# Turning the keys' lower parts of both attention maps together, and moving the scale and parts of w_o's last block

## The chip, the cores and the metric

The kernel runs on one core of one Trainium2 chip. The metric is the device time of one execution in microseconds (us), as the median of several runs.

## The reference

One step of a hybrid encoder layer: 1024 new frames of a prompt and 32 frames of a running stream (with 512 cached keys and values) go through differential attention and retention, are merged and multiplied with w_o, and pass a gated feed-forward and a gated per-layer embedding. D_MODEL is 1024, there are 8 heads of each kind. Each attention head has two maps of width 64. What matters here:

```python
def mix_inputs(x, w_in, g_norm, g_qn, g_kn, pos):
    h = rmsnorm(x, g_norm)
    z = h @ w_in
    qa, ka, va, qr, kr, vr, g_ret, gate_a, gate_r = jnp.split(z, splits, axis=-1)
    qa = rmsnorm(qa.reshape(B, T, A_HEADS, 2, A_DIM), g_qn)
    ka = rmsnorm(ka.reshape(B, T, A_HEADS, 2, A_DIM), g_kn)
    ...

def diff_attn_prompt(qa, ka, va, lam):
        s = jnp.einsum('bqhcd,bkhcd->bhcqk', q_blk, ka).astype(jnp.float32) * scale
        p = jax.nn.softmax(jnp.where(mask, s, -jnp.inf), axis=-1)
        a = p[:, :, 0] - lam * p[:, :, 1]
        return jnp.einsum('bhqk,bkhe->bqhe', a.astype(va.dtype), va)

def merge_and_tail(x, o_a, o_r, gate_a, gate_r, p, w_o, g_ffn, w_ff_gate, w_ff_up,
                   w_ff_down, g_ple, w_ple, w_ple_gate):
    mix = jax.nn.sigmoid(gate_a) * o_a + jax.nn.sigmoid(gate_r) * o_r
    x = x + mix @ w_o
    h = rmsnorm(x, g_ffn)
    x = x + (jax.nn.silu(h @ w_ff_gate) * (h @ w_ff_up)) @ w_ff_down
    gate = jax.nn.sigmoid(rmsnorm(x, g_ple) @ w_ple_gate)
    return x + gate * (p @ w_ple)
```

## The kernel before

All large products are made of fp16 pairs: a matrix is scaled and split into a high part and a lower part (value minus high part), and a product is high x high, high x low and low x high, added up in PSUM (`mm3`, L473). The tokens are 1056 columns, in 9 tiles (8 of 128 and one of 32).

**Stage A** runs over 8 heads x 9 tiles. For each unit it projects the tile (L734 to L736, 24 products of 512 columns for each of two weight pairs), and `unit_a` (L1011) takes queries and keys of both maps. It normalises them, casts the high parts to fp16 (L1060, L1061), subtracts for the lower parts (L1063, L1064), turns six 128x128 groups on PE into one PSUM bank (L1072) and copies them out: four groups with the keys to `kT` (L1077) and two with the queries to `q4` (L1081; both in the helper at L388). Group 0 and 1 hold a map's high and lower query parts side by side, so one product over 128 rows multiplies both with the keys' high part, which stands twice in the rows (64 rows each); a second product with the keys' lower part (L878) completes the scores. For this the kernel keeps `kT[:, 0:2]` (high parts of the two maps, doubled) and `kT[:, 2:4]` (lower parts, doubled), and so for the 512 cached keys in `kcs` (L846 to L854). `attend` (L864) makes scores, softmax and the product with the values; `unit_b` (L1182) makes retention and the merged rows.

**The seam.** In the last head, `load_ple`, `load_wo_0` and `load_wo_1` load the per-layer embedding's and w_o's weights: w_o in four blocks of 256 columns (0 and 1 in one weight tile, 2 and 3 in another). `load_block_steps` (L392) loads a block to one of two staging tiles, takes four reductions for the largest value (L426), multiplies by the rows' scale and reduces again (L429, L435), lets PE turn the column of maxima and spread it (L275, L286 in `spread_max`), and derives the scale. `split_block` (L449) then makes the parts, eight pairs of one ACT and one DVE instruction (L459, L461). For block 3 the kernel stops after the scale (`hold`), and the split is done in the next stage. Beside this run the products of the per-layer embedding (PLE, L474 to L476 into `pj`, copied out at L1354 and stored at L1360 and L1362).

**Stage BC** (`stream_bc`, L1796) first makes the products with w_o: four chunks of tokens (352, 352, 176, 176 columns) x 8 column blocks m of 128, each 8 x 3 products. `residual` (L1540) loads `xf` by DMA (L1546), adds each product to it (L1553), stores it, sums squares (L1561, L1564), and makes the norm (PE at L1572 and L1587, then L1591) and the operands of the feed-forward (L1501, L1507, and the sums for a product scheme of 7 in place of 8). `load_gu` (L1613) prepares the feed-forward's weights. Then come gate and up, the down product, and at last the embedding's gate.

**What sets the order.** PE, DVE, ACT and POOL execute in the order in which the program issues, and that order is made by a planner (`Flow`, L86), one for stage A and one for the products with w_o and what follows. Each piece of work is a generator that yields its estimated cost on an engine: `V(n)` is 0.07 + n/960 us on DVE, `S(n)` 0.1 + n/1200 us on ACT, `M(us)` a fixed time on PE. The planner always issues the item that can start first; with equal starts, the lower `prio` goes first. A result reaches another engine after 0.13 us (`LAT`), and an item for PE that doesn't follow one on PE is planned 0.3 us later (`MARGIN`). `("delay", us)` pushes an item back, `("get", key)` and `("put", key)` take and free a buffer, `("wait", key)` waits for `("set", key)`. The second planner starts again at 0. DMAs are issued by SP, outside this order. The hardware then executes each engine's list in order and waits where data are late, whatever the plan said.

## Time and profile before

| | us |
|---|---|
| median of 3 runs (1913.74 to 1914.2) | 1914.16 |
| the profiled execution | 1914.65 |
| its span, first to last instruction | 1912.8 |
| PE busy in the span | 1860.5 |
| DVE busy | 1503.2 |
| ACT busy | 1091.3 |
| POOL busy | 681.9 |

The granted clock of TensorE was 0.998 of full speed on average. In the rows, L12 is line 12 of the kernel before; out<-in names the tiles; PE is the matmul row, PEld the load of weights, which overlaps. A row of the timeline gives the start in us, the duration in us, the engine and the instruction, and in brackets how long the engine was idle before it and what ended that. Matmuls are pipelined: the next one starts before the one before it has ended, so the distance between starts is the time that one takes from the next.

### The profile page before, as it was taken

Reading aid. Unit: us, or ns where it says so; the run is one execution under the profiler, and the core shown is the slowest. Engines: PE = TensorE matmul, PEld = TensorE weight load, DVE = VectorE, ACT = ScalarE, POOL = GpSimd, SP = SyncE. Lnnn points to the kernel's source line nnn. Section 1 sums busy time; section 2 is a strip of 40 time slices with the busy share of each in tenths; the row PEclk is TensorE's granted clock in tenths of the full one; section 3 lists DMA queues with packets and bytes.
Section 4 is the critical chain, followed back from the end, with each engine's and each line's share of the span. In section 5 each row is a group of like instructions: output and inputs, shape, how many; then the busy total and the mean of one; then the engine's idle time right before and its main releaser. Section 6 shows DMA issues by size and latency. Waiting matters only on the chain.

```text
span 1912.8 us, 38341 instructions
## 1 busy us (share of the span) xinstructions
PE 1860.5 (97%) x14183; PEld 1217.9 (64%) x14183; DVE 1503.2 (79%) x3955; ACT 1091.3 (57%) x2863; POOL 681.9 (36%) x1162
## 2 busy tenths in 40 slices
PE   7899999999999999999999998999999999999999
PEld 3556565555655566555556685777777776666665
DVE  7888888788787787777887589999999986654364
ACT  7777667677676776767656345655555552101132
POOL 3654444445444544544442067232232300000010
PEclk9999999999999999999999999999999999999999
DMA  5122112122021111211215610222111116112031
GB/s 192 71 72 78 60 32 82 36 57 81 26 68 58 50 64 34 80 59 30 85 34 191 222 65 29 101 83 87 65 59 63 50 53 262 62 61 79 11 133 50
DMA packets 71806, 146.91 MB, mean 77 GB/s; under 512 B 25249, under 2 KB 52001, under 8 KB 63682
## 3 DMA queue, kind: packets, MB, share of 16 engines
q1 hardware_dynamic: 71618, 144.46, 22.5%
q8 instruction: 111, 1.82, 0.4%
q14 instruction: 77, 0.63, 0.1%
HBM read 113.09 MB, written 31.34 MB: 76 GB/s over the span
## 4 chain that ended last, share of the span: by engine, by line
PE 70%; DVE 15%; POOL 6%; ACT 5%; issue 2%; DMA 1%; SPq 0%; POOLq 0%; ACTq 0%; DVEq 0%
PE ps L474 9%; PE ps L475 9%; PE ps L476 9%; PE pj L734 7%; PE pj L735 7%; PE pj L736 7%; PE ps L1478 4%; PE ps L1477 4%; PE ps L1476 4%; DVE nm L885 2%; ACT p L895 2%; DVE w L467 1%; POOL qkr L770 1%; PE sc L875 1%; PE sc L878 1%
## 5 line engine op out<-in xcount | busy, mean ns | idle before, releaser
L734 PE MATMUL pj<-w,xh 128*128 128x512 f16 x1024 | 388.9, 380 | 2.8 <-ACT w L465 2.8
L735 PE MATMUL pj<-w,xh 128*128 128x512 f16 x1024 | 389.0, 380 | 0.6 <-DVE w L467 0.6
L736 PE MATMUL pj<-w,xh 128*128 128x512 f16 x1024 | 389.0, 380 | 0.0
L475 PE MATMUL ps<-mixs,w 128*128 128x352 f16 (+1 forms) x960 | 260.6, 277 | 1.8 <-POOL mixs L1501 1.8
L474 PE MATMUL ps<-mixs,w 128*128 128x352 f16 (+1 forms) x960 | 260.7, 277 | 0.3 <-ACT pws L1354 0.3
L476 PE MATMUL ps<-mixs,w 128*128 128x352 f16 (+1 forms) x960 | 260.5, 277 | 0.0
L474 PEld LDWEIGHTS <-w 128*128 128x128 f16 x1728 | 169.7, 98 | 58.8 <-issue 5.1
L476 PEld LDWEIGHTS <-w 128*128 128x128 f16 x1728 | 169.5, 98 | 56.6 <-issue 5.6
L475 PEld LDWEIGHTS <-w 128*128 128x128 f16 x1728 | 169.5, 98 | 50.1 <-issue 1.3
L736 PEld LDWEIGHTS <-xh 128*128 128x128 f16 x1024 | 100.2, 98 | 122.3 <-issue 1.9
L1610 POOL TENSOR_TENSOR st<-st 128x512 f32<-128x512 f32 x66 | 86.2, 1305 | 250.7 <-DVE w L1605 186.6
L734 PEld LDWEIGHTS <-xh 128*128 128x128 f16 x1024 | 101.4, 99 | 76.7 <-issue 3.7
L735 PEld LDWEIGHTS <-xh 128*128 128x128 f16 x1024 | 100.2, 98 | 74.6 <-issue 3.7
L895 ACT ACTIVATE p<-sc,nb,scs 128x256 f32<-128x256 f32 (+7 forms) x128 | 106.6, 833 | 71.7 <-POOL nb L887 49.1
L475 PE MATMUL ps<-tT,w 128*128 128x352 f16 (+1 forms) x528 | 143.6, 277 | 3.5 <-DVE tT L1501 3.5
L476 PE MATMUL ps<-tT,w 128*128 128x352 f16 (+1 forms) x528 | 143.7, 277 | 0.0
L474 PE MATMUL ps<-tT,w 128*128 128x352 f16 (+1 forms) x528 | 143.6, 277 | 0.0
L1605 DVE SCALAR_TENSOR_TENSOR w<-st,gus,w 128x512 f16<-128x512 f32 x132 | 140.7, 1067 | 0.1
L885 DVE TENSOR_REDUCE nm<-sc 128x2 f32<-128x256 f32 (+6 forms) x112 | 102.9, 918 | 19.5 <-PE sc L878 18.3
L1478 PE MATMUL ps<-a,w 128*128 128x352 f16 x312 | 97.5, 313 | 0.5 <-DVE w L1696 0.5
L1476 PE MATMUL ps<-a,w 128*128 128x352 f16 x312 | 97.5, 313 | 0.0
L1477 PE MATMUL ps<-a,w 128*128 128x352 f16 x312 | 97.5, 312 | 0.0
(432 smaller groups left out, 4874.4 us busy)
## 6 DMA issues: line engine op xcount, KB each, us to landing
st<-in_win_dram SPq DMA_DIRECT2D x30, 1024.0 KB, 4.8
st<-in_wgu_dram SPq DMA_DIRECT2D x22, 1024.0 KB, 4.9
st<-in_wdn_dram SPq DMA_DIRECT2D x16, 704.0 KB, 4.5
out_dram<-kv SPq DMA_DIRECT2D x64, 128.0 KB, 1.7
a_d<-a SPq DMA_DIRECT2D x9, 528.0 KB, 2.6
b<-a_d SPq DMA_DIRECT2D x9, 528.0 KB, 7.1
mixs<-mix_d SPq DMA_DIRECT2D x8, 528.0 KB, 7.0
pw_d<-pws SPq DMA_DIRECT2D x12, 352.0 KB, 5.1
```

The costliest lines, as they stand in the source:

```text
L474: nc.tensor.matmul(out=ps, lhsT=wh, rhs=ah, start=first, stop=False)
L475: nc.tensor.matmul(out=ps, lhsT=wh, rhs=al, start=False, stop=False)
L476: nc.tensor.matmul(out=ps, lhsT=wl, rhs=ah, start=False, stop=last)
L734: nc.tensor.matmul(out=ps, lhsT=xhi, rhs=w[:, k, 0], start=(k == 0), stop=False)
L735: nc.tensor.matmul(out=ps, lhsT=xhi, rhs=w[:, k, 1], start=False, stop=False)
L736: nc.tensor.matmul(out=ps, lhsT=xh[:, k, 1, t0:t0 + P], rhs=w[:, k, 0], start=False, stop=(k == KD - 1))
L885: nc.vector.tensor_reduce(out=nm[0:R, mc], in_=pv, axis=AX.X, op=ALU.max, negate=True)
L895: nc.scalar.activation(pt[0:R, 0:NK], ps[0:R, p0:p0 + NK], AF.Exp, bias=nb[0:R, m:m + 1], scale=sc_ap[0:R], accum_out=Z[0:R, m:m + 1])
L1476: nc.tensor.matmul(out=ps, lhsT=wt[:, 0, j], rhs=a[:, 0, cs], start=(first and j == js[0]), stop=False)
L1477: nc.tensor.matmul(out=ps, lhsT=wt[:, 1, j], rhs=a[:, 0, cs], start=False, stop=False)
L1478: nc.tensor.matmul(out=ps, lhsT=wt[:, 2, j], rhs=a[:, 1, cs], start=False, stop=(last and j == js[-1]))
L1605: nc.vector.scalar_tensor_tensor(out=w[:, i, 1], in0=src, scalar=s, in1=w[:, i, 0], op0=ALU.mult, op1=ALU.subtract)
```

## The change

In `unit_a` the lower parts of both maps' keys are cast once, not doubled, and stand side by side in one group: five groups are turned instead of six. The turned group holds map 0's lower part in rows 0 to 63 and map 1's in rows 64 to 127. `kT[0:64, 2]` and `kT[64:128, 3]` take them by two copies of 64 partitions each, and the other halves of `kT[:, 2]` and `kT[:, 3]` are zeros, written once at the start. `kcs` has the same form, and is one tile for all heads now, with its zeros. The score products are as before in number and shape.

For w_o's block 3, stage A only issues the DMA. Maximum, scale and parts are made in stage BC by `last_wo`. The products with w_o are taken in another order: chunk 0's m 0 to 5, chunk 1's m 0, chunk 0's m 6 and 7 (the first that need block 3), then the rest of chunk 1, chunk 2 and chunk 3. The loads of the first gate/up weights and of chunk 2's residual are added after chunk 0's last product, as before.

```diff
@@ -389,7 +389,7 @@
 
     at = [0]
 
-    def load_block_steps(src, w, b, gi, tag, rowf, out, tail=False, due=None, late=None, hold=None):
+    def load_block_steps(src, w, b, gi, tag, rowf, out, tail=False, due=None, late=None):
 
 
         yield ("get", "st")
@@ -441,9 +441,6 @@
             nc.vector.tensor_scalar(out=sk, in0=rowf, scalar1=s, scalar2=None, op0=ALU.mult)
         if late is not None:
             w = yield from late()
-        if hold is not None:
-            hold.update(st=st, sk=sk)
-            return
         yield from split_block(w, b, st, s, None if rowf is None else sk, due)
 
     def split_block(w, b, st, s, sk, due=None):
@@ -517,7 +514,12 @@
         ps_o = pa.enter_context(DT(name="ps_o", bufs=3, space=PSUM))
 
         cs_sb = hp.tile([P, NT, 2, 32], F32, name="cs_sb")
+
         kT = hp.tile([P, 4, T], F16, name="kT")
+        kcs = hp.tile([P, 4, PAST], F16, name="kcs")
+        for t in (kT, kcs):
+            nc.gpsimd.memset(t[64:128, 2], 0.0)
+            nc.gpsimd.memset(t[0:64, 3], 0.0)
         vh = hp.tile([P, NT, 2, P], F16, name="vh")
         oa = hp.tile([P, NQ, P], F32, name="oa")
 
@@ -843,14 +845,14 @@
             nc.vector.tensor_tensor(out=vsc, in0=dA[1], in1=s[:, 1:2], op=ALU.mult)
             if h:
                 yield ("wait", ("av", h - 1, NT - 1))
-            kcs = hp.tile([P, 4, PAST], F16, tag="kcs", name="kcs")
             vcs = hp.tile([P, 4, 2, P], F16, tag="vcs", name="vcs")
             for m in range(2):
                 yield ("prio", 2 if due - at[0] > FAR else -2)
                 yield S(512, 0.08)
                 nc.scalar.activation(kcs[:, m], kc[:, m], AF.Copy, scale=s[:, 0:1])
                 yield V(512, 1.0, 0.06)
-                nc.vector.scalar_tensor_tensor(out=kcs[:, 2 + m], in0=kc[:, m], scalar=s[:, 0:1], in1=kcs[:, m],
+                ms = slice(64 * m, 64 * m + 64)
+                nc.vector.scalar_tensor_tensor(out=kcs[ms, 2 + m], in0=kc[ms, m], scalar=s[ms, 0:1], in1=kcs[ms, m],
                                                op0=ALU.mult, op1=ALU.subtract)
             yield S(512, 0.08)
             nc.scalar.activation(vcs[:, :, 0], vc, AF.Copy, scale=s[:, 1:2])
@@ -1054,27 +1056,31 @@
 
             yield ("get", "qst")
             yield S(384, 0.1)
-            st = wk.tile([P, 6, 2, 64], F16, tag="qst", name="qst")
+            st = wk.tile([P, 5, 2, 64], F16, tag="qst", name="qst")
             zqk = z[0:R].rearrange("p a (m c) -> p a m c", m=2)
             sf = st[0:R].rearrange("p g a c -> p (g a) c")
             nc.scalar.copy(sf[:, 0:4:3], zqk[:, 0])
             nc.scalar.copy(st[0:R, 2:4], zqk[:, 1].unsqueeze(2).broadcast_to([R, 2, 2, 64]))
-            yield V(384, 1.0, 0.07)
+            yield V(256, 1.0, 0.07)
             nc.vector.tensor_tensor(out=sf[:, 1:3], in0=zqk[:, 0], in1=sf[:, 0:4:3], op=ALU.subtract)
-            nc.vector.tensor_tensor(out=st[0:R, 4:6], in0=zqk[:, 1].unsqueeze(2).broadcast_to([R, 2, 2, 64]),
-                                    in1=st[0:R, 2:4], op=ALU.subtract)
+            nc.vector.tensor_tensor(out=st[0:R, 4], in0=zqk[:, 1], in1=st[0:R, 2:4, 0], op=ALU.subtract)
             yield ("put", "z")
             yield ("get", "o")
-            yield M(0.336)
+            yield M(0.28)
             pt = ps_o.tile([P, 1024], F16, tag="o", name="t")
-            ptv = pt[:, 0:768].rearrange("p (g c) -> p g c", g=6)
-            for g in range(6):
+            ptv = pt[:, 0:640].rearrange("p (g c) -> p g c", g=5)
+            for g in range(5):
                 nc.tensor.transpose(out=ptv[:, g, 0:R], in_=st[0:R, g].rearrange("p a c -> p (a c)"), identity=id16[0:R, 0:R])
             yield ("put", "qst")
             if h and i < NT - 1:
                 yield ("wait", ("s", h - 1, NT - 2))
-            g = yield either(V(512, 0.5), S(512, -0.09))
-            copy(g, kT[:, :, t0:t0 + RT], ptv[:, 2:6, 0:RT])
+            g = yield either(V(256, 0.5), S(256, -0.07))
+            copy(g, kT[:, 0:2, t0:t0 + RT], ptv[:, 2:4, 0:RT])
+
+            for m in range(2):
+                g = yield either(V(128, 0.5), S(128, -0.06))
+                ms = slice(64 * m, 64 * m + 64)
+                copy(g, kT[ms, 2 + m, t0:t0 + RT], ptv[ms, 4, 0:RT])
             yield ("get", "q4")
             g = yield either(V(256, 0.5), S(256, -0.07))
             q4 = wk.tile([P, 2, P], F16, tag="q4", name="q4")
@@ -1284,17 +1290,18 @@
             yield ("wait", "ple")
 
             def late():
-                if j == 0:
-                    yield ("get", "w")
-                    tail["wos"][1] = pair_tile()
-                    yield ("set", "wo1")
-                yield ("wait", "wo1")
+                yield ("get", "w")
+                tail["wos"][1] = pair_tile()
                 tail["wos"][1][1][j] = d[j]
                 return tail["wos"][1][0]
             d = [None, None]
             if j:
-                tail["hold"] = {}
-            yield from load_block_steps(wo[2 + j], None, j, None, "o", mixun, d, late=late, hold=tail["hold"] if j else None)
+                yield ("get", "st")
+                tail["hold"] = stage()[:, 0:KD * 256].rearrange("p (k c) -> p k c", k=KD)
+                yield DM(1.0)
+                nc.sync.dma_start(out=tail["hold"], in_=wo[2 + j])
+                return
+            yield from load_block_steps(wo[2 + j], None, j, None, "o", mixun, d, late=late)
 
         def load_ple():
 
@@ -1793,19 +1800,45 @@
                     banks[j, p, n] = ps
                     yield ("set", ("pp", j, p, n))
 
+            def last_wo():
+
+                st = tail["hold"]
+                yield ("delay", 3.0)
+                am8 = sm(8, "wam81", 1)
+                for q in range(4):
+                    yield V(512)
+                    nc.vector.tensor_reduce(out=am8[:, 2 * q:2 * q + 2], in_=st[:, 2 * q:2 * q + 2], axis=AX.X, op=ALU.max,
+                                            apply_absolute_value=True)
+                yield V(8)
+                nc.vector.tensor_tensor(out=am8, in0=am8, in1=mixun, op=ALU.mult)
+                yield V(4)
+                am = sm(1, "wam", 3)
+                nc.vector.tensor_reduce(out=am, in_=am8, axis=AX.X, op=ALU.max)
+                yield ("delay", 2.0)
+                s, d = yield from weight_scale(am, 1, None, "o1", False, at_bank=("ss", pss))
+                wos[1][1][1] = d
+                yield V(8)
+                sk = sm(KD, "wsk1", 1)
+                nc.vector.tensor_scalar(out=sk, in0=mixun, scalar1=s, scalar2=None, op0=ALU.mult)
+                yield from split_block(wos[1][0], 1, st, None, sk)
+                yield ("set", "wo1")
+
             def stream_bc():
-                flow.add(split_block(wos[1][0], 1, tail["hold"]["st"], None, tail["hold"]["sk"]), 0)
+                flow.add(last_wo(), 0)
                 flow.add(residual(0), 0)
                 flow.add(residual(1), 0)
-                for c in range(NW):
-                    if c == 1:
+
+                for c, ms_ in ((0, range(6)), (1, range(1)), (0, range(6, KD)), (1, range(1, KD)), (2, range(KD)), (3, range(KD))):
+                    if (c, ms_[0]) == (1, 1):
                         flow.add(load_gu(0), 2)
                         flow.add(load_gu(1), 2)
                     if c == 3:
                         flow.add(load_gu(2), 2)
-                    if c in (1, 2):
+                    if (c, ms_[0]) in ((1, 1), (2, 0)):
                         flow.add(residual(c + 1), 0)
-                    for m in range(KD):
+                    for m in ms_:
+                        if (c, m) == (0, 6):
+                            yield ("wait", "wo1")
                         yield ("get", "ps")
                         yield M(1.83 if c > 1 else 3.6)
                         ps = bank_w(c)
```

## Rows read from the trace of the kernel before

**Rows 1.** The page: busy time, share of span, instructions of each engine.

```profile
PE 1860.5 (97%) x14183; PEld 1217.9 (64%) x14183; DVE 1503.2 (79%) x3955; ACT 1091.3 (57%) x2863; POOL 681.9 (36%) x1162
```

**Rows 2.** Stretches: us, busy PE, PEld, DVE, ACT, POOL, clock, DMA, GB/s.

```profile
480.00:528.00 48.00, 47.92 (x393) 30.12 (x392) 36.74 (x103) 31.63 (x94) 23.14 (x51) 1.00 0.10 28
...
1104.00:1128.00 24.00, 24.00 (x255) 20.62 (x254) 17.39 (x34) 7.97 (x19) 10.56 (x10) 1.00 0.29 98
1128.00:1208.00 80.00, 65.43 (x604) 51.78 (x602) 78.28 (x163) 45.43 (x111) 57.34 (x61) 0.96 0.14 46
```

**Rows 3.** PE's waits from 50 to 1054 us: total us, times, longest us.

```profile
PE t L1237 <- DVE aT L935: 2.0, 3, 0.7
...
PE sc L875 <- ACT th L1198: 1.1, 3, 0.4
...
PE sc L875 <- ACT p L895: 0.7, 3, 0.3
...
PE t L1072 <- DVE xh L719: 0.2, 1, 0.2
```

**Rows 4.** Timeline of PE: a unit's six transpositions and what follows.

```profile
502.15 0.50 PE L1072 MATMUL t<-id,qst 128*128 128x128 f16 x6
502.48 0.38 PE L734 MATMUL pj<-w,xh 128*128 128x512 f16 x1
```

**Rows 5.** Timeline of PE: one wait in two places of stage A.

```profile
601.47 0.33 PE L1237 MATMUL t<-cst_sb,mx 128*128 128x128 f32 x1 [0.67 <-DVE aT L935]
...
849.13 0.33 PE L1237 MATMUL t<-cst_sb,mx 128*128 128x128 f32 x1 [0.68 <-DVE aT L935]
```

**Rows 6.** Line 388, copies: duration ns min/median/max, first and last start, forms.

```profile
L388 DVE COPY kT<-t x57: 209/415/426, 53.0 to 991.1; 128x512 f16<-128x512 f16 x50, 128x128 f16<-128x128 f16 x7
L388 DVE COPY q<-t x46: 274/281/292, 68.3 to 1001.4; 128x256 f16<-128x256 f16 x46
L388 ACT COPY q<-t x26: 372/373/434, 47.8 to 991.9; 128x256 f16<-128x256 f16 x26
...
L388 ACT COPY kT<-t x15: 266/586/625, 45.2 to 1000.1; 128x512 f16<-128x512 f16 x14, 128x128 f16<-128x128 f16 x1
```

**Rows 7.** Groups by line and form: busy us, mean ns, idle before.

```profile
L1064 DVE TENSOR_TENSOR qst<-z,qst 128x256 f16<-128x256 f32 x72 | 30.5, 424 | 0.1
...
L1063 DVE TENSOR_TENSOR qst<-z,qst 128x128 f16<-128x128 f32 x72 | 21.3, 296 | 2.6 <-ACT qst L1060 2.2
```

**Rows 8.** Timeline of DVE at the seam.

```profile
1045.12 2.46 DVE L426 TENSOR_REDUCE wam<-st 128x2 f32<-128x512 f32 x4
1048.82 0.69 DVE L426 TENSOR_REDUCE wam<-st 128x2 f32<-128x512 f32 x1 [1.25 <-DMA st<-in_wo_dram]
...
1050.09 0.15 DVE L435 TENSOR_REDUCE wam<-wam 128x1 f32<-128x8 f32 x1
```

**Rows 9.** Timeline of PE at the seam, to w_o's second block of products.

```profile
1049.26 0.31 PE L476 MATMUL pj<-w 128*128 128x352 f16 x1
1050.30 0.27 PE L275 MATMUL mt<-cst_sb,wam 128*1 128x128 f32 x1 [0.72 <-DVE wam L435]
...
1054.40 0.31 PE L474 MATMUL ps<-mixs,w 128*128 128x352 f16 x1 [0.34 <-ACT pws L1354]
...
1057.98 0.31 PE L474 MATMUL ps<-mixs,w 128*128 128x352 f16 x1
```

**Rows 10.** Timeline of SP's queue: the issue of the first two xf.

```profile
1054.83 1.85 SPq L1546 DMA_DIRECT2D xf<-in_xT_dram  x2
```

**Rows 11.** Timeline of DVE after the seam.

```profile
1055.01 4.83 DVE L461 SCALAR_TENSOR_TENSOR w<-st,wsk,w 128x256 f16<-128x256 f32 x12
1064.57 0.58 DVE L1553 SCALAR_TENSOR_TENSOR xf<-ps,o0d,xf 128x352 f32<-128x352 f32 x1 [4.72 <-DMA xf<-in_xT_dram]
```

**Rows 12.** Timeline of POOL at the start.

```profile
1.37 0.53 POOL L533 MEMSET suz<- 128x512 f32 x1
...
8.01 0.26 POOL L769 TENSOR_SCALAR xss<-xss 128x1 f32<-128x1 f32 x1 [5.74 <-ACT xsq L689]
```

## The prediction, made before the change was run

> **What bounds the kernel now.** I read the page's busy shares first: PE is busy for 97% of the span [rows 1]. A busy PE row is not yet a full PE, so I then read the start times of matmuls in the timeline, and the busy time of every engine by stage. In stage A (the attention and retention stage, up to 1054 us) one 512-column product follows the other every 0.215 us, and all that PE waited in that stage after 50 us is a list of 18 entries that add up to 15.6 us, from 2.0 down to 0.2 [rows 3]. So a matmul taken out of stage A is time taken out of the span, as long as DVE and ACT keep up; in a typical stretch they are busy for 36.7 and 31.6 of 48 us [rows 2]. The products with w_o (1054 to about 1145 us) leave PE full too, as between 1104 and 1128 us [rows 2]. Then, from 1128 to 1208 us, DVE is the bound: 78.3 of 80 us busy, while PE is idle for 14.6 us [rows 2]. So three things are to be asked: what PE loses or gains in stage A, what happens at the seam near 1054 us, and whether DVE's full stretch begins later.
>
> **Part 1: one transposition less per tile.** The change turns the two heads' lower key parts in one 128x128 transposition instead of two. Six of them take 0.33 us from the first one's start to the start of what follows [rows 4], 0.055 us each. (One lasts 0.22 us by itself, but they overlap in the array, so the start-to-start time is what the path pays.) There are 8 heads x 9 tiles = 72 units: 72 x 0.055 = 4.0 us out of PE's order in stage A. The score products keep their number and shape; the lower operand is now half zeros and costs the same columns.
>
> DVE loses half of its second subtraction: L1064 took 424 ns for 256 columns, the same operation with 128 columns (L1063) took 296 ns [rows 7], 0.128 us per unit. In exchange the one copy of four groups becomes three copies. On DVE it took 415 ns; a copy of two groups takes 281 ns and one of 128x128 took at least 209 ns, so 281 + 2 x 209 = 699 ns, 0.28 us more [rows 6]. On ACT 586 ns become 373 + 2 x 266 = 905 ns, 0.32 us more [rows 6]. Net per unit: 0.16 us on DVE or 0.19 us on ACT, 11 to 14 us over the stage, if every nanosecond counted. Consecutive instructions overlap (in the DVE queue of the seam, four reductions of 0.68 us end after 2.46 us [rows 8], 0.08 us shared at each step), so two more instructions per unit cost some 0.12 us instead of 0.28 in throughput, about what the shorter subtraction gives back. Cover: the idle 11 us in 48 on DVE [rows 2]. I put the load at 0. What remains is latency: the first score product of a unit comes some 0.3 us later after the transpositions. Among PE's 18 entries only two name a score product (L875), and they wait for ACT's exponent and tanh, not for a key copy [rows 3]. The planner also knows of the three copies (its costs 0.20 + 2 x 0.14 instead of 0.34 us, plus 0.13 us per hand-over) and sets other work between. I take 0, with 0 to 12 us as the bounds.
>
> [...]
>
> A new order of costs makes the planner lay the stage out anew. The waits that are left come back in each pair of heads: the same 0.67 us wait stands at 601.5 and at 849.1 us, 247.7 us apart [rows 5]. So any wait that the new order adds or drops counts about four times. From 15.6 us over some four such periods, that is 3.9 us per period; I let a period change by up to 1 us, so 4 us to either side, centred on 0.
>
> The zeros are set once by four memsets on POOL. After its memsets at the start POOL waits 5.74 us for its next work [rows 12]; a memset of 128x512 f32 took 0.53 us, and the four new ones write 64 rows of 1056 or 512 fp16 values, which I bound by four times that, 2.1 us: hidden. If they weren't, 2 us at the start would be lost. The cache's lower part on 64 instead of 128 partitions keeps its 512 columns: 0.
>
> **Part 2: w_o's last scale and parts go among w_o's products.** What is removed from the seam: the four reductions of block 3, its scale and its way over PE. Before, DVE met the first of these reductions at 1048.82, after waiting 1.25 us for its DMA, ahead of the two small operations that finish block 2's maximum; that came at 1050.09 [rows 8], and PE, which needed it for its transposition, started at 1050.30 what could have started 0.15 us after 1049.26: 0.89 us lost [rows 9]. Without block 3 in the queue block 2's maximum is ready before 1048. Gain 0.9 us; all that follows starts earlier by that (bounds 0.5 to 1.1: behind it the PLE outputs wait for their banks). The DMA of block 3 stays where it was in SP's order, ahead of PLE's last stores.
>
> What is added: the reductions now stand in the second planner's DVE order. By its costs the first two are planned for 3.0 and 3.7 us after the stage's start, the first residual (L1553) becomes ready at 4.03 us and goes third, and reductions three and four behind it. But the planner gives the residual no wait for its DMA, and in the trace L1553 waits for xf until 1064.57, 10.2 us after w_o's first product at 1054.40 [rows 9, 11]; xf's DMA was issued at 1054.83 [rows 10]; by the code it stands behind PLE's stores. In the kernel before, the same L1553 stood behind twelve split instructions, with nothing behind it that PE needed soon [rows 11]. Now, behind it: 0.5 us for L1553, two reductions at 0.6 us, two small operations, a hand-over: 2.2 us. So the maximum reaches PE 12.4 us after the start. PE's transposition of it is planned for 9.03 us and so stands behind the third block of products; a block takes 1057.98 - 1054.40 = 3.58 us [rows 9], three take 10.7 us. PE, strictly in order, stands 1.7 us, and all products behind it with it. Bounds 0 (xf lands 2 us earlier) to 4 us (lands 2 us later). The second PE step stands a block later, with DVE done by then. The eight parts then end some 25 us after the start, and the first product that needs them comes after seven blocks and the stand, 27 us: hidden by 1 to 2 us.
>
> Also, chunk 0's last two products move behind chunk 1's first: chunk 0's norm and the weights of gate/up start one block, 3.6 us, later, while chunk 1 ends where it did. DVE idles 6.6 us of the 24 us between 1104 and 1128 [rows 2], which takes that in. If none of it did, DVE's full stretch would begin 3.6 us later. Nearest to the first: I take 0.5 us, bounds 0 to 3.6.
>
> **Sum.** The profiled execution took 1914.65 us, 0.49 us above the median of the runs shown. 1914.65 - 4.0 - 0.9 + 1.7 + 0.5 = 1911.95, that is about 1911.5 us as a median.
>
> **Rivals.** *No new wait* (faster): xf lands before PE needs the maximum, or the transposition is placed a block later, and DVE's stretch takes in the shifted norm: 1914.16 - 4.0 - 0.9 = 1909.3 us; with one wait of a us less per pair of heads 1905.3. For it: only 2 us decide, and they hang on one DMA among others. Against: L1553's row is plain.
>
> *The saving is given back* (no change): PE is not the bound where it seems, and its 4 us come back as waits for units that DVE, ACT and POOL release no earlier. 1914.16 - 0.9 + 1.7 + 0.5 = 1915.5 us. Against it: 15.6 us of waits in 1000 us. This is also the case in which the change doesn't do what it is for.
>
> *Three copies in series* (slower): the fixed part of two more copies stands on the way from the transpositions to the score products, and PE, in order, waits it out. 0.16 to 0.19 us x 72 = 11.5 to 13.7 us; with the rest of the sum, 1911.5 + 11.5 to 13.7 = 1923 to 1925 us. It makes the kernel slower by over 0.2% from 1918.0 - 1911.5 = 6.5 us on, when some 40 of 72 units pay it in full. Against it: no row shows PE waiting for a key copy now [rows 3].
>
> **How the numbers follow.** A measurement of this kernel can tell about 0.2%, 3.8 us, from no change: 1910.3 and 1918.0 us are the borders. The forecast has 0.46, with 1909 to 1915 as its own range, 0.08 of it below 1910.3. No new wait 0.30, all faster. Given back 0.13, all the same. Copies in series 0.11, slower. So faster 0.38, same 0.51, slower 0.11. The range from 1906 to 1918 leaves out about 0.1 above and 0.05 below, and takes in the bounds of xf's landing and of the planner's new order.
>
> **What would show it.** Five transpositions per tile with 0.28 us to the next start; PE's waits in stage A again near 15 us, none of them on L388; w_o's first product 4 to 6 us earlier than 1054.40. Then a wait of PE of 1 to 2.5 us at the transposition of block 3's maximum, three blocks later, behind an L1553 that waits for xf. The distance from w_o's first product to the end of the span should grow by about 2 us. I am wrong if PE's waits in stage A grow by more than 4 us, if L875 waits for the copies, or if PE's idle time from 1128 to 1208 changes by more than 3 us.

## The result, and the profile after

The changed kernel takes 1916.57 us (median of 20 runs, 1913.28 to 1918.37) against 1914.18 us (1913.04 to 1914.61, 20 runs): a ratio of 1.0013, 95% interval [1.0007, 1.0019]. The forecast was 1911.5 us, 2.7 us faster; the change is 2.4 us slower, and its runs are spread over 5 us where the kernel before spreads over 1.6. Its profiled execution took 1914.81 us (span 1912.9), 1.8 us under its median, so what is read from this trace explains the trace first, and the median only with the runs further down.

The page of the kernel after, busy time by engine (answers [rows 1]):

```profile
PE 1860.0 (97%) x14111; PEld 1212.6 (63%) x14111; DVE 1514.9 (79%) x4017; ACT 1109.0 (58%) x2947; POOL 674.7 (35%) x1164
```

The stretches of after that answer to [rows 2], same columns:

```profile
480.00:528.00 48.00, 47.71 (x387) 29.77 (x386) 37.58 (x108) 32.02 (x99) 18.75 (x42) 1.00 0.07 19
1104.00:1128.00 24.00, 24.00 (x256) 20.67 (x255) 19.69 (x37) 9.18 (x21) 13.99 (x13) 1.00 0.27 90
1128.00:1208.00 80.00, 65.01 (x602) 51.46 (x600) 78.27 (x163) 45.32 (x111) 57.21 (x61) 0.96 0.14 46
```

72 matmuls are gone, DVE is busy for 11.7 us more and ACT for 17.7 us more. PE's waits from 50 to 1054 us (answers [rows 3]; all 14 entries add up to 14.1 us, where 18 added up to 15.6):

```profile
PE t L1243 <- DVE mx L1238: 3.2, 10, 0.7
PE t L1243 <- DVE aT L937: 1.4, 4, 0.5
PE por L1169 <- DVE inn L1167: 1.4, 4, 0.6
PE sc L877 <- ACT p L897: 1.3, 4, 0.5
...
PE pr L1161 <- DVE qT L388: 1.1, 2, 0.7
PE ps L471 <- ACT pws L1361: 1.1, 1, 1.1
...
PE sc L877 <- ACT q L388: 0.6, 1, 0.6
```

The seam, in the timelines of after; first PE (answers [rows 9]; L471 is w_o's first product):

```profile
1052.66 0.31 PE L471 MATMUL ps<-mixs,w 128*128 128x352 f16 x1 [1.07 <-ACT pws L1361]
...
1064.46 0.27 PE L275 MATMUL mt<-cst_sb,wam 128*1 128x128 f32 x1 [0.91 <-DVE wam L1816]
```

ACT ahead of that first product:

```profile
1051.66 0.51 ACT L456 ACTIVATE w<-st,wsk 128x256 f16<-128x256 f32 x1 [0.74 <-DVE wsk L441]
1052.07 0.54 ACT L1361 ACTIVATE pws<-pj,pled 128x352 f32<-128x352 f32 x1
```

DVE (answers [rows 8, 11]; L1810 to L1816 are block 3's maximum, L1560 is the residual):

```profile
1053.61 1.28 DVE L1810 TENSOR_REDUCE wam<-st 128x2 f32<-128x512 f32 x2 [1.99 <-DMA st<-in_wo_dram]
...
1062.24 0.58 DVE L1560 SCALAR_TENSOR_TENSOR xf<-ps,o0d,xf 128x352 f32<-128x352 f32 x1 [4.19 <-issue]
1062.74 1.27 DVE L1810 TENSOR_REDUCE wam<-st 128x2 f32<-128x512 f32 x2
...
1064.25 0.16 DVE L1816 TENSOR_REDUCE wam<-wam 128x1 f32<-128x8 f32 x1
```

And SP's queue, the issue of the first two xf (answers [rows 10]):

```profile
1053.08 2.14 SPq L1553 DMA_DIRECT2D xf<-in_xT_dram  x2
```

Three things are to be seen. The last product of stage A's last projection starts at 1023.27 us, 1.67 us before its counterpart in before (1024.94), not 4.0. w_o's first product comes 1.74 us earlier (1052.66 against 1054.40): the 0.9 us of the seam did not arrive, since the product now waits 1.07 us for the last PLE output, which stands in ACT's order behind the first cast of block 2. And the new wait is where the prediction put it: L1560, which starts 0.17 us after the first xf has landed (1062.07 us), stands ahead of reductions 3 and 4, and PE waits at the transposition of block 3's maximum. The third block of w_o's products takes 4.76 us in place of 3.58 us, the fourth, with the rest of the scale's steps on PE among its products, 3.99 us. That spends 1.59 of the 1.74 us, and at the end of DVE's full stretch (1128 to 1208 us) the changed kernel is 0.1 us behind.

### The profile page after: what moved, and what is told of

The parts are those of the page before. It is cut to its first block, busy times and chain, and to the rows that moved or that the text cites. A ratio compares the mean times of both kernels' runs of the same rounds, so it can differ in the third digit from the quotient of the medians.

```text
span 1912.9 us, 38379 instructions
## 1 busy us (share of the span) xinstructions
PE 1860.0 (97%) x14111; PEld 1212.6 (63%) x14111; DVE 1514.9 (79%) x4017; ACT 1109.0 (58%) x2947; POOL 674.7 (35%) x1164
## 5 line engine op out<-in xcount | busy, mean ns | idle before, releaser
L471 PE MATMUL ps<-mixs,w 128*128 128x352 f16 (+1 forms) x960 | 260.6, 277 | 1.1 <-ACT pws L1361 1.1
L471 PEld LDWEIGHTS <-w 128*128 128x128 f16 x1728 | 169.8, 98 | 58.7 <-issue 5.2
L471 PE MATMUL ps<-tT,w 128*128 128x352 f16 (+1 forms) x528 | 143.6, 277 | 0.0
L887 DVE TENSOR_REDUCE nm<-sc 128x1 f32<-128x640 f32 (+6 forms) x112 | 102.9, 919 | 19.7 <-PE sc L880 18.7
```

The source lines that it names most:

```text
L471: nc.tensor.matmul(out=ps, lhsT=wh, rhs=ah, start=first, stop=False)
L887: nc.vector.tensor_reduce(out=nm[0:R, mc], in_=pv, axis=AX.X, op=ALU.max, negate=True)
```

## The experiments

All shifts are read against the trace of before: "projection" is the start of the last product of stage A's last projection (1024.94 us), "w_o" the start of w_o's first product (1054.40 us). "Against before" is the difference of the medians on the same chip. The names e1 to e9 are those that expectations use. A shift comes from one trace and carries about 1 us: the changed kernel, the same once more and the same with the residual planned later have one order of stage A and show -1.67, -2.53 and -2.65 us. The intervals of the ratios leave 1.1 to 2.6 us to either side of a difference of the medians.

| kernel | projection, us | w_o, us | median, us | against before, us | ratio, 95% |
|---|---|---|---|---|---|
| after (profiled) | -1.67 | -1.74 | 1916.57 | +2.4 | 1.0013 [1.0007, 1.0019] |
| part 1 alone (e1) | -1.64 | +6.41 | 1923.69 | +10.1 | 1.0050 [1.0038, 1.0063] |
| part 2 alone (e2) | -1.17 | -1.92 | 1915.62 | +2.0 | 1.0010 [1.0001, 1.0019] |
| after, once more (e3) | -2.53 | -2.60 | 1916.19 | +2.6 | 1.0015 [1.0006, 1.0024] |
| after, residual planned later (e4) | -2.65 | -1.74 | 1913.28 | -0.3 | 0.9999 [0.9990, 1.0008] |
| part 1, old order (e5) | +2.56 | +3.59 | 1918.15 | +4.2 | 1.0021 [1.0012, 1.0030] |
| the same and part 2, residual later (e6) | +3.25 | +4.48 | 1919.08 | +5.1 | 1.0026 [1.0016, 1.0035] |
| part 1, old order, six transpositions (e7) | +4.57 | +4.90 | 1920.40 | +6.4 | 1.0032 [1.0019, 1.0044] |
| before, seven transpositions (e8) | +1.61 | +2.04 | 1916.65 | +2.7 | 1.0015 [1.0006, 1.0024] |
| before, five transpositions (it leaves out the sixth, so its keys' parts are not the right ones) | -3.17 | -2.12 | 1912.49 | -2.0 | 0.9991 [0.9982, 1.0000] |
| part 1, old order, queries first (e9) | +3.50 | +4.52 | 1919.09 | +4.6 | 1.0025 [1.0015, 1.0035] |
| the same with a mask | +0.54 | +2.18 | 1916.33 | +1.9 | 1.0010 [1.0001, 1.0019] |
| before, 2 copies more on DVE (PSUM) | +10.23 | +11.63 | 1926.42 | +12.3 | 1.0067 [1.0054, 1.0079] |
| before, 2 copies more on ACT (PSUM) | +18.93 | +20.32 | 1935.44 | +21.3 | 1.0111 [1.0097, 1.0124] |
| before, 2 copies more on ACT (SBUF) | +2.70 | +2.94 | 1917.68 | +3.1 | 1.0016 [1.0007, 1.0025] |
| before, 2 copies more on DVE (SBUF) | +2.90 | +2.64 | 1917.75 | +3.2 | 1.0017 [1.0008, 1.0026] |
| before, planned with cheaper transpositions | -3.02 | -0.89 | 1913.99 | -0.2 | 0.9999 [0.9990, 1.0008] |
| before, planned with cheaper subtractions | +1.45 | +3.41 | 1919.23 | +5.1 | 1.0026 [1.0016, 1.0036] |
| after, residual later, queries first | -7.90 | -5.28 | 1912.07 | -2.4 | 0.9987 [0.9979, 0.9996] |

**The parts alone.** Part 1 alone is the change without the new `last_wo` and with w_o's loading as before.

> Part 1 alone (five transpositions, three key copies), w_o's block 3 as before. Theory 'xf wait': the loss and the wide spread of the changed kernel come from part 2, where block 3's maximum waits for xf's landing; part 1 alone then takes 1912 to 1913.5 us (the 1.7 us that stage A ended earlier in the profile, at most), and its runs lie within 2 us as those before. Rival 'stage A': the three copies make stage A's waits vary; then part 1 alone takes 1915 to 1917 us with runs 4 to 5 us apart.

Part 2 alone is the other half of the diff.

> Part 2 alone (block 3's scale and parts among w_o's products), six transpositions as before. 'xf wait': 1915 to 1918 us and runs 4 to 5 us apart, with a wait of PE at the transposition of block 3's maximum of 1 to 5 us. 'Stage A': 1914 us within 0.7 us, runs within 2 us.

The changed kernel again, on the same chip:

> The changed kernel once more, for a second profile and its spread: both theories expect 1916.6 us with runs some 5 us apart. 'xf wait' expects the wait of PE at block 3's maximum (1.07 us in the first profile, of a run at 1914.81 us) to be longer by as much as this profiled run is slower. 'Stage A' expects that wait unchanged and w_o's first product later.

And the changed kernel with one line more, after the residual's wait for w_o's products:

```
+ if (c, m) == (0, 0):
+     yield ("delay", 6.5)
```

> The changed kernel, with the planner told that the first residual can't start before xf has landed (a delay of 6.5 us), so that block 3's four reductions stand ahead of the first residual in DVE's order. 'xf wait': PE's wait at block 3's maximum is gone (under 0.3 us), the runs lie within 2 us, and the median is 1913 to 1914 us. 'Stage A': as the changed kernel, 1916 to 1917 us, runs 5 us apart.

Part 1 alone was a miss of 10 us. In its new order block 3's first reduction stands ahead of the two small operations that finish block 2's maximum, waits for its DMA, and PE with it. PE's row at the seam:

```profile
1056.65 0.37 PE L275 MATMUL mt<-cst_sb,wam 128*1 128x128 f32 x1 [6.46 <-DVE wam L435]
```

and DVE's:

```profile
1055.18 0.69 DVE L426 TENSOR_REDUCE wam<-st 128x2 f32<-128x512 f32 x1 [6.96 <-DMA st<-in_wo_dram]
```

It is the 0.89 us of [rows 8, 9], seven times as long, and PE's granted clock was 0.50 behind it (columns as in [rows 2]; the clock is the third number from the end):

```profile
1054.00:1058.00 4.00, 1.35 (x6) 0.72 (x7) 2.82 (x8) 0.00 (x0) 0.00 (x0) 0.50 1.04 387
...
1062.00:1066.00 4.00, 4.00 (x15) 2.07 (x14) 4.00 (x11) 3.96 (x10) 0.00 (x0) 0.50 0.97 341
```

At a granted clock of 0.50 w_o's first block took 6.48 in place of 3.58 us. The projection's -1.64 us, the 8.05 us lost from there to w_o and these 2.90 us make 9.3 of the 10.1 us. So part 2 takes away a hazard whose size the plan sets. Part 2 alone came out as the xf wait would have it (1915.62 us, with a wait of PE of 1.34 us at block 3's maximum), but its runs spread over 2.4 us and not over 4 to 5. The last two kernels settle the wait behind xf: PE's row at the wait, in the changed kernel run once more:

```profile
1064.99 0.27 PE L275 MATMUL mt<-cst_sb,wam 128*1 128x128 f32 x1 [2.29 <-DVE wam L1816]
```

The stretches around it in the same run:

```profile
1062.00:1066.00 4.00, 1.71 (x11) 0.91 (x10) 2.60 (x7) 0.99 (x2) 0.00 (x0) 0.94 0.50 182
1066.00:1070.00 4.00, 4.00 (x19) 2.20 (x17) 1.72 (x4) 0.50 (x1) 0.00 (x0) 0.63 0.85 233
```

The same stretches with the residual planned later:

```profile
1062.00:1066.00 4.00, 4.00 (x29) 2.63 (x28) 2.31 (x5) 0.99 (x2) 0.00 (x0) 1.00 0.89 279
1066.00:1070.00 4.00, 4.00 (x28) 2.56 (x26) 2.78 (x12) 2.00 (x5) 0.00 (x0) 1.00 1.06 369
```

In the changed kernel run once more xf landed at 1062.59 us, 0.52 us later than in the first profile, though w_o had started 0.86 us earlier; PE stood 2.29 us instead of 0.91 and then ran at a granted clock of 0.63: the third block took 6.15 us and the fourth 5.66 us, 4.65 us over two plain blocks, of which 0.5 us are the steps of block 3's scale (the same blocks take 3.69 and 3.98 us in the kernel without the wait). The first profile lost 1.59 us there; the 3.06 us more, less the 0.86 us of the earlier start, are 2.20 us, and the two executions differ by 2.19 us (1917.00 and 1914.81). With reductions 3 and 4 done at 1059.36, before xf lands at 1062.21, there is no wait, the clock stays at 1.00, and the median falls by 2.9 us, to that of before; the runs lie within 2.1 us again (1912.35 to 1914.47). So the wait, and the clock behind it where xf is late, cost 2.9 us of the median. That they are all of the added spread is not shown: part 2 alone has the wait too, without that spread.

**Transpositions and copies in the old order.** For these kernels the planner was given the old costs, so PE's order is that of before, but for the transpositions themselves. First part 1's instructions as they are in the diff, the three copies under one planned cost:

```
  yield M(0.336)
  ...
- copy(g, kT[:, :, t0:t0 + RT], ptv[:, 2:6, 0:RT])
+ copy(g, kT[:, 0:2, t0:t0 + RT], ptv[:, 2:4, 0:RT])
+ for m in range(2):
+     ms = slice(64 * m, 64 * m + 64)
+     copy(g, kT[ms, 2 + m, t0:t0 + RT], ptv[ms, 4, 0:RT])
```

> Part 1's instructions (five transpositions, the shorter subtraction, three copies of keys, kcs' lower half on 64 partitions) in the order of the kernel before: the planner is given the old costs, so the order of PE differs from before only by the 72 transpositions that are left out, and w_o is as before. My theory (PE bounds stage A, the copies are hidden, what the change lost was the new order of the seam and of stage A): 72 x 0.055 us = 4.0 us less, 1909.6 us by the median of before in the last batch (1913.6), ratio 0.998. Rival 'the saving is given back' (PE waits for units that DVE and ACT release no earlier): 1913 to 1914 us, ratio 1.000. Rival 'three copies in series': 1917 us or more.

then with part 2 and the later residual, as a candidate for a better kernel:

> The changed kernel with two things mended: the planner gets the old costs for part 1, and the first residual is planned 6.5 us later, so that nothing that PE needs stands behind its wait for xf. My theory: e5's 4.0 us plus part 2 without the wait (0.9 us at the seam less some 0.5 us for the shifted norm): 1909 to 1910 us, ratio 0.9975. If the saving of stage A is given back: 1913 us as the changed kernel with the residual mended alone (1913.3).

The first came out where its rival of the three copies in series stood (1917 us or more), and the second is no better kernel: it takes 0.9 us more, which the intervals don't tell apart from nothing. Its first product with w_o waits 1.67 us for a PLE output on DVE. Then part 1's copies and subtraction with six transpositions:

```
- for g in range(5):
-     nc.tensor.transpose(out=ptv[:, g, 0:R], in_=st[0:R, g]...)
+ for g in range(6):
+     nc.tensor.transpose(out=ptv[:, g, 0:R], in_=st[0:R, min(g, 4)]...)
```

> As the kernel with part 1's instructions in the old order, but with a sixth transposition (the fifth's tile a second time, not read): the price of the three copies and the shorter subtraction alone, with PE's work as before. My theory (hidden, latency only): 1913.6 us, ratio 1.000, so 4.0 us above e5. Copies in series: 3 to 13 us above before. If PE doesn't bound stage A, e7 and e5 take the same time.

before with seven (`range(7)` and `min(g, 5)` in the same lines):

> The kernel before with a seventh transposition per tile (the sixth a second time, not read), order and costs as before: what a transposition costs where nothing else changes. My theory: 72 x 0.055 us = 4.0 us more, 1917.6 us, ratio 1.002. If PE's order has room for it (the saving is given back): under 1 us more.

and before with five:

```
- for g in range(6):
+ for g in range(5):
  ...
- copy(g, kT[:, :, t0:t0 + RT], ptv[:, 2:6, 0:RT])
+ copy(g, kT[:, :, t0:t0 + RT], ptv[:, 1:5, 0:RT])
```

> The kernel before with the sixth transposition left out and nothing else: the one copy of four groups takes groups 1 to 4 in place of 2 to 5, so the keys' parts are wrong. Order, copies and subtractions are as before. Theory of the prediction: 72 x 0.055 = 4.0 us less, 1910 us. Theory after the run with a seventh transposition (+2.7 us, 0.029 us each along stage A, the rest absorbed by waits that end by themselves): 2 to 2.5 us less, 1911.5 to 1912 us.

A transposition takes 0.055 us in PE's order in each of these traces (first start to the next product: 0.28, 0.34 and 0.39 us for five, six and seven). Yet 72 more shift the projection by 1.61 us and the end by 2.7 us, and 72 fewer by 3.17 and 2.0 us: 0.02 to 0.04 us each. Without the first four units, whose start differs from one execution to the next, 2.1 and 2.6 of 3.7 us arrive between the fifth unit's transpositions and the last's; and the two kernels with part 1's copies differ by 2.25 us in the median for five and six. So half to two thirds of a transposition's time arrives. And part 1's copies, with PE's work unchanged, lose 4.57 us at the projection and 6.4 us in all, as the rival of the copies in series had it (3 to 13 us). One unit shows a part of how. PE in the kernel with part 1 in the old order:

```profile
368.07 0.39 PE L879 MATMUL sc<-kT,q 128*128 128x512 f16 x1 [0.77 <-DVE q L388]
```

DVE ahead of it:

```profile
366.80 0.63 DVE L388 COPY kT<-t 128x256 f16<-128x256 f16 x3
...
367.72 0.29 DVE L388 COPY q<-t 128x256 f16<-128x256 f16 x1
```

The three copies of keys hold DVE for 0.67 us (366.80 to 367.47) where the one held it for 0.32 us, the queries' copy stands behind them, and PE waits. The same product in before:

```profile
368.38 0.39 PE L875 MATMUL sc<-kT,q 128*128 128x512 f16 x1 [0.38 <-ACT th L1198]
```

It waited there too, and the trace named ACT's tanh, which ended at 368.35 us, 0.04 us after the queries' copy. So I first took the latency for the cause, and moved the queries' copy ahead of the two short ones:

```
  copy(g, kT[:, 0:2, t0:t0 + RT], ptv[:, 2:4, 0:RT])
+ kg = g
  ...
  copy(g, q4[:, :, 0:R], ptv[:, 0:2, 0:R])
+ for m in range(2):
+     ms = slice(64 * m, 64 * m + 64)
+     copy(kg, kT[ms, 2 + m, t0:t0 + RT], ptv[ms, 4, 0:RT])
```

> The kernel with part 1's instructions in the old order of PE (the one that took 1918.2 us, 4.2 above before), with the queries' copy moved ahead of the two copies of the keys' lower parts. PE's order is unchanged. In the trace of the former, PE waits ahead of a score product 27 times, 8.5 us in all, against 8 times and 2.5 us in before. Theory (the two additional copies stand ahead of the queries' copy, which PE's first score product needs): the queries come 0.1 us earlier than in before, the lower keys in time for the second product; the waits fall to some 2.5 us and the time by 6 us to 1912 us, ratio 0.999. Rival (DVE's and ACT's additional load as such is what costs, wherever the copies stand): 1917 to 1918 us.

That theory fell: 1919.1 us, no faster. PE's waits ahead of score products show a part of why. Part 1 in the old order (50 to 1054 us; total us, times, longest us):

```profile
PE sc L879 <- DVE q L388: 2.9, 6, 0.8
...
PE sc L879 <- ACT p L899: 1.0, 3, 0.4
...
PE sc L879 <- ACT q L388: 1.0, 3, 0.3
```

The same with the queries first:

```profile
PE sc L879 <- ACT p L899: 3.5, 8, 1.0
...
PE sc L879 <- DVE q L388: 0.5, 3, 0.2
```

The 3.9 us of waits for queries became 0.5, and the waits for ACT's exponent rose from 1.0 to 3.5 us. DVE does the same work, only in another order, and the maximum from which the exponent is made comes out of the same queue; that it is this link that moved the wait is argued, not shown.

The traces show the rest start for start. The kernels with before's order issue the same 6774 products between the first and the last of the projections, apart from the transpositions, and the start of each can be set against its start in before. What the distance grows by at the score products, at the products right behind the transpositions and at all others (us):

| kernel | behind the transpositions | score products | all others | sum |
|---|---|---|---|---|
| before, five transpositions | -3.96 | +0.78 | +0.26 | -2.92 |
| before, seven transpositions | +4.22 | -0.62 | -2.29 | +1.31 |
| part 1, old order, six transpositions | -0.89 | +5.35 | +0.44 | +4.90 |
| part 1, old order | -4.85 | +6.22 | +1.60 | +2.97 |
| the same, queries first | -4.84 | +3.45 | +5.15 | +3.76 |
| the same with a mask | -4.85 | +3.38 | +2.24 | +0.77 |
| before, 2 copies more on DVE (PSUM) | -0.09 | +2.56 | +7.74 | +10.21 |

With the copies as in the diff nearly all of the loss arises at the score products: there the copies did stand in series. With the queries first 2.8 us of it are gone, but 3.6 us more arise at other products, so what the order won was lost again elsewhere.

The next kernel adds a mask of ones and zeros and, where `kg` is DVE, takes this in place of the two copies:

```
+ nc.vector.tensor_tensor(out=kT[:, 2:4, t0:t0 + RT],
+                         in0=ptv[:, 4, 0:RT].unsqueeze(1).broadcast_to([P, 2, RT]),
+                         in1=msk.broadcast_to([P, 2, RT]), op=ALU.mult)
```

> As the kernel with the queries' copy first in the old order, and where the key copies run on DVE, the two copies of the lower parts are one product of the transposed tile with a mask of ones and zeros, 256 columns. Theory (what counts is when the queries and the lower keys come, and their order has mended that): the same time as that kernel within 1 us. Rival (the number of instructions on DVE counts): 1 to 2 us below it.

One instruction less per unit on DVE (a product with a mask in place of two copies, in the 57 of 72 units whose keys DVE copies) gives back 2.8 us. In the table above this gain isn't at the score products (3.45 and 3.38) but at the others (5.15 and 2.24). So this part goes by DVE's load and not by the way from the transpositions to the score products.

**Load by itself.** Two copies of no use per tile, in before's order. From the transposed tile, behind the queries' copy (with "S" for ACT):

```
  copy(g, q4[:, :, 0:R], ptv[:, 0:2, 0:R])
+ dmy = wk.tile([P, P], F16, tag="dmy", name="dmy")
+ for ms in (slice(0, 64), slice(64, 128)):
+     copy("V", dmy[ms, 0:R], ptv[ms, 5, 0:R])
```

> The kernel before, its order unchanged, with two more copies of 64x128 per tile on DVE, behind the queries' copy, into a tile that nothing reads: additional load of DVE that stands on no way from the transpositions to the score products. If DVE's load as such costs (as the run with the queries' copy first says, which won nothing, and the one with the mask, which won 2.8 us by one instruction less): 72 x 2 x 0.21 to 0.24 us start to start are 30 us of DVE, of which I expect a sixth to a third to arrive, 5 to 10 us: 1919 to 1924 us. If only the latency ahead of the score products costs: under 1.5 us, 1914 to 1916 us.

> The same two additional copies on ACT. ACT is busy for 31.6 of 48 us in stage A, DVE for 36.7. If the load of the fuller engine is what costs: under half of what the copies on DVE cost, 1915 to 1918 us. If latency alone costs: under 1.5 us.

and from the staged tile, ahead of the keys' copy, the parts that the copying engine wrote itself (`st[0:R, a, 1 - a]` for DVE):

```
+ dmy = wk.tile([P, P], F32, tag="dmy", name="dmy")
+ for a in (0, 1):
+     copy("S", dmy[0:R, 64 * a:64 * a + 64], st[0:R, a, a])
  yield ("put", "qst")
```

> The kernel before, its order unchanged, with two more copies of 128x64 per tile on ACT, from the staged keys and queries (written by ACT itself) into a tile that nothing reads: ACT's additional load without a wait for another engine. The earlier run with two additional copies on ACT lost 21 us, but there ACT also had to wait for DVE's copies out of the same bank, 16 us in all. If ACT's load as such is what cost: over 12 us again, more than the same on DVE. If the added wait was what cost: 5 to 10 us, and no more than the same on DVE.

> The same two additional copies on DVE, from the parts that DVE itself wrote. By the earlier run with two additional copies on DVE (10.2 us at the last projection for 144 copies of 0.21 us start to start, a third of their time): again about a third of the time added, 6 to 12 us. If only the latency ahead of the score products counted, and not DVE's load: under 3 us.

On DVE the first pair adds 0.48 us per unit start to start, 34 us, and 10.2 us arrive at the projection; the second pair adds 0.20 us, 14 us, and 2.9 us arrive. On ACT the second pair adds 0.28 us, 20 us, and 2.7 us arrive. So a seventh to a third of the time added to either engine arrives, although from 50 to 1020 us DVE is idle for 19% and ACT for 30%. My figures for the second pairs were too high on both engines (5 to 10 and 6 to 12 us, against 3.1 and 3.2 us in the median), and on DVE the result lies at the bound of the rival that only latency counts (under 3 us). The second pair stands ahead of the keys' copy, where DVE waits for PE's transpositions (12.8 us in before, 10.1 us with the pair), so a part of it falls into that wait. It is the first pair that shows a price of load. The 18.9 us of the first pair on ACT, where I had expected less than on DVE, are for the most part no price of load: in that run ACT's added copies waited for DVE's copy of the queries out of the same tile. ACT's waits in stage A have the row (total us, times, longest us):

```profile
ACT dmy L388 <- DVE q L388: 16.4, 26, 2.0
```

What makes the one copy wait for the other there is not shown. Of the two readings of that run the added wait, 16.4 us, explains the larger part, as far as the row and the second pair tell: the second pair's copies waited for nothing from 480 to 728 us, where the first pair's waited 4.2 us for DVE's. The second pair is shorter than the first (ACT is busy for 19.8 and 35.4 us more), so the split isn't exact.

**A new order by itself.** Before's instructions with one planned cost changed, `M(0.336)` to `M(0.28)` at the transpositions, or `V(384, 1.0, 0.07)` to `V(256, 1.0, 0.07)` at the subtractions:

> The kernel before with the planner's cost of the six transpositions at 0.28 in place of 0.336 us: the same instructions, laid out anew. It shows what a new order is worth by itself. The prediction took up to 1 us per pair of heads, 4 us to either side: the last projection's start within 4 us of before's 1024.9. If a new order is worth more (as the 6 us between the two kernels with the residual planned later, whose copies stand in another order, let one suspect): 4 to 8 us away from it. The whole time may move by up to 8 us besides, as the seam is laid out anew too.

> The kernel before with the planner's cost of the two subtractions as for 256 in place of 384 columns: the same instructions in a third order. As for the kernel with the cost of the transpositions changed: the last projection's start within 4 us of 1024.9 if a new order is worth what the prediction took, 4 to 8 us away if it is worth more.

The same instructions move the projection by -3.0 and +1.5 us and the median by -0.2 and +5.1 us. My bounds for stage A, 4 us to either side, hold for these two; up to w_o's first product the seam moves them by 2.1 and 2.0 us more.

**A faster version.** The changed kernel with the later residual, and the two short copies, each with its own planned cost, moved behind the queries' copy:

> The changed kernel with the first residual planned 6.5 us later and the queries' copy ahead of the two copies of the keys' lower parts, all known to the planner, which lays stage A out anew. If both of the changed kernel's losses are named rightly (2.9 us for the wait behind xf; the waits ahead of the score products, 4.4 us against 2.5 in before): 1910 to 1912 us, with 4 us to either side for the new order of stage A. If the copies cost by their load: 1913 us or more.

It takes 1912.07 us, ratio 0.9987 [0.9979, 0.9996]: 2.4 us under before on its chip, where the change was 2.4 us over it. Its 7.9 us at the projection are 5.3 us more than in the kernel whose copies stand as in the diff, and outside my bounds of 4 us for a new order. The order of the copies alone won nothing, so I take most of it for a lucky plan; no run separates the two. Of the 7.9 us, 2.6 us are lost ahead of w_o and 1.3 us in its first block (4.86 in place of 3.58 us), whose products start 0.29 us apart for 2.3 us and then 0.15 us; the granted clock was 0.88 from 1040 to 1054 us. The DMAs' busy share is 0.98 in that stretch (columns as in [rows 2]):

```profile
1040.00:1054.00 14.00, 10.77 (x64) 6.54 (x63) 7.69 (x25) 6.83 (x15) 0.00 (x0) 0.88 0.98 326
```

ACT's last PLE outputs wait for the stores ahead of them:

```profile
1047.23 1.00 ACT L1360 ACTIVATE pws<-pj,pled 128x352 f32<-128x352 f32 x2 [3.96 <-DMA pw_d<-pws]
```

and PE for ACT:

```profile
1049.12 0.45 PE L471 MATMUL ps<-mixs,w 128*128 128x352 f16 x1 [3.23 <-ACT pws L1360]
```

## Why the prediction was wrong

**What bounds stage A: the step that failed first.** I read PE's busy share and its 15.6 us of waits [rows 1, 3] as "a matmul taken out is time taken out, as long as DVE and ACT keep up". One view that I did not use says otherwise: the chain of work that ended last. Its shares of the whole span by engine, from the page of before:

```profile
PE 70%; DVE 15%; POOL 6%; ACT 5%; issue 2%; DMA 1%; SPq 0%; POOLq 0%; ACTq 0%; DVEq 0%
```

Of the 970 us from 50 to 1020 us PE has 58%, added up over the chain's pieces. A piece of that chain (start us, us, what):

```profile
594.26 1.08 ACT p L895 x2
595.35 0.61 ACT w L465
...
597.02 0.94 POOL orr L770
...
599.00 0.46 DVE z L1043
...
600.76 0.67 DVE aT L935
...
601.47 0.33 PE t L1237
```

And the busy times in the stretch (columns as in [rows 2]):

```profile
593.50:601.50 8.00, 7.33 (x39) 3.64 (x37) 7.08 (x22) 5.20 (x16) 5.68 (x10) 1.00 0.38 125
```

For 8 us the path runs over ACT, POOL and DVE, and shows on PE only as the wait of 0.67 us at its end [rows 5]; meanwhile PE is busy for 7.33 us with products that it has in stock. So a busy PE is not the same as a path over PE: PE holds 58% of the chain in stage A, not 97%. That in such stretches a shorter PE only waits longer is argued, and at this place it isn't so: the wait is 0.67 us in the kernels with five and with seven transpositions too.

```profile
599.31 0.33 PE L1237 MATMUL t<-cst_sb,mx 128*128 128x128 f32 x1 [0.67 <-DVE aT L935]
```

With five, 0.78 of the 1.04 us that are given back up to the last projection arise at the score products. Nor is the share in the chain a price: it is 75% in the kernel planned with cheaper transpositions, whose median is before's. What the runs show is the size: of 4.0 us of PE half to two thirds arrive, and work added to DVE alone makes the stage longer. The list of waits was too short a measure besides. It counts a wait from the end of the product before, and a projection product lasts 0.38 us [rows 4] while the next starts after 0.215, so that a stand of 0.16 us isn't in it.

**The transpositions, 4.0 us.** The 0.055 us each were right (five take 0.28 us to the next start, as predicted). What arrives is 2.0 us of the time for 72 fewer (interval 0 to 3.4), and 2.7 and 2.25 us by the other two comparisons: half to two thirds of the term.

**The copies, taken at 0 with bounds 0 to 12.** This is the term that was furthest off: 6.4 us in the old order, at the middle of the bounds. "Sets other work between" and "hidden" were the wrong steps: in that order nearly all of the loss stands in series at the score products (+5.35 us there, -0.45 us at all other products up to the last projection), as the slower rival said, at about half its price. The sign of being wrong that I had named, a score product waiting for the copies, is there too: 3.9 us in part 1 in the old order. It isn't this place alone, since with the queries first the time didn't fall. In the changed kernel itself the planner gives 118 of the 216 copies of keys to DVE and 98 to ACT, and the waits of one for the other's copies out of the same tile come to 19.2 us against 10.2 in before; what that costs is not shown. The slower rival had the sign right, and short copies do cost more per column here: on DVE 256 columns took 281 ns, 68% of the 415 ns of 512 columns [rows 6]. Taken as path time, the longer copies less the shorter subtraction gave 11.5 to 13.7 us, about twice what the run shows. "No row shows PE waiting for a key copy" was true and misled: a wait names only the last of its releasers, as the 0.04 us between the queries' copy and ACT's tanh above show.

**Stage A as a whole.** -2.0 and +6.4 would make +4.4; part 1 in the old order takes +4.2. The planner, told the new costs, wins that back and more: the changed kernel reaches the last projection 1.67 to 2.65 us before its counterpart. How much of this is its knowledge of the costs and how much a plan as lucky as that of cheaper transpositions (-3.0) can't be told apart here. PE's waits are near 15 us as predicted (14.1) and show nothing of it: with 4.0 us taken out and 1.67 us won, PE stood 2.3 us more, while the list fell by 1.5 us. That none would be on L388 was wrong by two entries, 0.6 us for queries and 1.1 us for retention's. The transposition that is left out turned two maps of one head, not two heads, as the prediction has it; its sum doesn't change.

**The seam, 0.9 us.** Block 2's maximum does come without the stand, but the term went into the next wait, 1.07 us for the PLE output. I had named this bound ("the PLE outputs wait for their banks") and not priced it.

**The wait behind xf, 1.7 us, bounds 0 to 4.** Mechanism, place and row were right. It measured 1.18 us in the profiled run (the third block's excess), 4.65 us with a granted clock of 0.63 behind it in the other, and 2.9 us between the medians. The size failed in two ways: the start of w_o came 1.7 and not 4.9 us earlier, and the wait of 2.29 us was followed by that clock, which the term had no place for.

**The shifted norm, 0.5 us.** In the trace of after DVE takes it in: 78.27 of 80 us as before, and 0.25 us are lost from 1109 to 1215 us.

**The sum and the rivals.** Forecast and median are 5.1 us apart. Stage A fell short by 1.4 to 2.3 us (4.0 less 2.65 or 1.67), the seam by 0.8, xf cost 1.2 us more, the steps of block 3's scale among w_o's products 0.4 us that were not in the sum, the norm 0.25 us less: 3.5 to 4.5 us. The rest, 0.6 to 1.6 us, can't be assigned; it is less than what a new plan moves. The nearest rival was "the saving is given back" (1915.5 us), which I had given 0.13: its reason, that PE's time comes back as waits for units that the other engines release no earlier, is what the runs with five and seven transpositions show, for a third to half of the saving. The one behind it (copies in series, 0.11) is what the old order shows for the copies. So the mechanisms of two rivals, both left out of the sum, were at work, each at about half its price.

## What to carry to other kernels

Where one engine is busy for 97% and in order, ask the chain of work, not the busy share, how much of the path lies on it: here 58% in stage A, and of 4.0 us taken off it 2.0 to 2.7 arrived, while work added to engines idle for a fifth to a third of the time cost a seventh to a third of its length. Set start against start too: that showed where the copies' time was lost, which the list of waits did not. Before a reduction, or anything that the bottleneck needs soon, is put in an engine's order, see what stands ahead of it there and waits for a DMA; planning that one instruction later gave back the change's 2.9 us here. And compare small edits under a fixed order: a planner that lays a stage out anew moved the same instructions by -0.2 to +5.1 us.

## What was not expected of the hardware

The granted clock fell behind some waits of PE and not behind others of the same length. It was 0.63 from 1066 to 1070 us behind the wait of 2.29 us, and 0.50 from 1054 to 1066 us behind the one of 6.46 us; behind the one of 3.23 us w_o's products were 0.29 us apart for 2.3 us and then 0.15 us; behind 0.91 us it stayed at 1.00. In the first and the third of these the wait and the slower products together cost 1.8 and 1.4 times the wait. But the wait of 3.07 us that before and part 1 in the old order both have at one place (1148.03 and 1151.62 us; PE's product at L300, for DVE) left it at 0.65 over the next 4 us in the one (first line) and at 1.00 in the other:

```profile
1148.03:1152.03 4.00, 4.00 (x19) 2.22 (x19) 4.00 (x13) 3.03 (x11) 3.98 (x6) 0.65 0.15 45
1151.62:1155.62 4.00, 3.76 (x25) 2.27 (x24) 4.00 (x13) 3.03 (x11) 3.98 (x6) 1.00 0.17 49
```

So the length of a wait doesn't say by itself what it costs. And the first xf, with the DMAs busy throughout (a share of 1.02 to 1.06 from 1054 to 1062 us), took 8.99 us from issue to landing in the one execution of the changed kernel and 10.37 us in the other, so that L1560 started 9.58 and 10.97 us after w_o's first product, 0.17 and 0.18 us after the landing.
